# Weight stripes of 512 columns, gates projected in the merge, and a delta net ahead of the attention, in a one-core transformer layer with expert retrieval

## The chip, the cores and the metric

The kernel runs on one core of one Trainium2 chip, as one program of 56,994 profiled instructions. The metric is the device time of one execution in microseconds. A core has five engines with queues of their own: TensorE (PE; its weight loads are listed as PEld), VectorE (DVE), ScalarE (ACT), GpSimd (POOL) and SyncE (SP, which here only issues DMAs). Each engine works off its instructions in a fixed order.

## The reference

One layer over 1024 tokens of width 1024, all in float32. `rmsnorm` stands ahead of each part, and each part is added to `x`.

```python
# 1. token mixing: one input projection, two branches, gates per channel
proj = rmsnorm(x) @ w_in                                   # 1024 x 5640
sb_q, sb_k, sb_v, g_q, g_k, g_v, g_z, g_b, g_a, gate_sb, gate_gdn = split(proj)
o_sb = stick_breaking_attention(sb_q, sb_k, sb_v)          # 8 heads x 64, causal
q, k, v = silu(causal_dwconv(g_q, g_k, g_v)); q, k = l2norm(q), l2norm(k)
o_g  = gated_delta_rule(q, k, v, sigmoid(g_b), decay(g_a)) # 4 heads x 128, chunks, a recurrence
o_g  = rmsnorm(o_g) * silu(g_z)
merged = sigmoid(gate_sb) * (o_sb @ w_sb_up) + sigmoid(gate_gdn) * (o_g @ w_gdn_up)
x = x + merged @ w_mix_out
# 2. cross-attention of 4 heads into 256 memory tokens
x = x + softmax_attention(rmsnorm(x) @ w_cq, rmsnorm(mem) @ w_ckv) @ w_co
# 3. PEER: per token and head the 16 best of 128 x 128 experts, 8 heads
expert, gate = two_stage_topk(rmsnorm(x) @ w_pq, subkeys)  # 128 expert slots per token
x = x + sum(gelu(peer_u[expert] . rmsnorm(x)) * gate * peer_v[expert])
return rmsnorm(x)
```

## The kernel before, in words

**Layout.** Activations are kept transposed, channels on partitions and tokens along the free dimension. A product in float32 is made of three: `split` writes a value as `hi + lo` in the tensor engine's fast float32 format (ACT copies `hi`, DVE or POOL subtracts to get `lo`), and `mm3` multiplies hi by hi, lo by hi and hi by lo, so 24 matmuls for a weight tile of 1024 x 128.

**Weights.** `proj` yields one product per 128 columns of a weight matrix: it loads the tile `raw` (512 KB, three buffers), splits it into `wh` and `wl` (two buffers each) and runs `mm3` into a PSUM tile `pj` (two buffers). The rows of such a tile are 512 bytes long in DRAM. `dense_h` does the same for the transposed expert matrix `peer_ut`.

**Groups.** The tokens go in three groups of 256, 384 and 384 (groups 0, 1, 2). For each group `token_mixing` comes first, then `cross`, then `routing`; the choice of experts (`choose`, long on DVE) follows with the next group's mixing. Inside `token_mixing` the order is: norm; 12 projections of the delta net with the short convolution; SiLU and l2 norm of q, k, v (a `yield` stands here, at which the choice of experts of the group before is put in); 12 projections of the attention (`qT`, `kT`, `vN`); the attention, `stick`, by blocks of 128 queries and 128 keys, two chains of four heads each; 20 projections for the gates, each passed through a sigmoid and stored to `gate_sc` in DRAM; the delta net's chunks (`Chunk.inverse`, `Chunk.scan`); in group 0 `memory_kv`; then the merge, which loads the gates back, lifts both branches (`w_sb`, `w_gdn`) and applies `w_mix`.

**Retrieval.** Of the eight blocks of 128 tokens five fetch their experts' rows by indirect DMAs of POOL, one 512 KB gather for each of 128 slots: `retrieve_u` (row times token on DVE), then `retrieve_v` (sums of rows on PE) or `retrieve_y` (sums on DVE). Seven `row` buffers hold the rows. Blocks 4, 5 and 6 use dense products over all 16,384 experts instead: `spread` turns the chosen gates into a matrix through one-hot tiles `o0`, `o1` (on DVE, and on POOL or ACT), `dense_ahead` makes the first 36 of 128 tiles of activations, and `dense` the rest and the products with `peer_v`. The gathers of later blocks run beside both.

**Order.** The program is written with pools and tiles; a planner with a cost model of its own orders the instructions on each engine ahead of the run, by priority in the order of the program, and puts in the waits. A pool that opens where another was closed waits for that one's tiles. What is written later can be ordered earlier where its operands and buffers are free: the gathers begin during group 1's mixing, the gate projections are spread over the attention.

Of the kernel before, what the change touches and what calls it, by code (L numbers as in the profile page):

```python
# [20 lines left out]
P = 128  # L21
# [5 lines left out]
SH_G, SH_R, SH_S, SH_Z = 3, 0, 6, 0  # L27
# [7 lines left out]
WLS = 2  # L35
SHS = 3
OBS = 12
# [14 lines left out]
def block_kernel(ctx: ExitStack, tc: tile.TileContext, x_t, mem_t, gains, cst, sel, eye, w_in, conv, a_log,  # L52
# [22 lines left out]
    # ---- small helpers  # L75
# [42 lines left out]
    def mix(a, b, ratio):  # L118
        """Steps of a and b in turn, ratio of a for each of b."""
# [21 lines left out]
    # ---- constants  # L141
    cs = const.tile([P, NCST, P], F32, name="cs")
    sp.dma_start(cs, cst)
# [29 lines left out]
    vec.tensor_copy(mk, cs[:, C_SB:C_SB + 2])  # L173
    trir = const.tile([P, 2, P], F32R, name="trir")
# [10 lines left out]
    # ---- scratch in DRAM  # L185
# [4 lines left out]
    gate_sc = dram.tile([len(GROUPS), 20, P, TMAX], F32, name="gate_sc")  # L190
# [35 lines left out]
    def proj(w, col0, ncol, hi, lo, n, kt=KD, share=0):  # L226
        """Yields (tile index, product) for each 128 columns of w, transposed: [columns, tokens]. GpSimd splits
        every share-th tile of w."""
        wv = w.rearrange("(k p) c -> p k c", p=P)
        for c in range(0, ncol, P):  # L230
            raw = wp.tile([P, KD, P], F32, name="raw", bufs=3)
            sp.dma_start(raw[:, :kt], wv[:, :, col0 + c:col0 + c + P])
            wh = wp.tile([P, KD, P], F32R, name="wh")
            wl = wp.tile([P, KD, P], F32R, name="wl", bufs=WLS)
            split(wh[:, :kt], wl[:, :kt], raw[:, :kt], eng=pool if share and c // P % share == share - 1 else vec)
            ps = j_tile()[:, :n]
            mm3(ps, wh, wl, hi, lo, kt)
# [26 lines left out]
    # ---- stick-breaking attention of one 128-query block, four heads at a time, keys on partitions  # L264
    def stick(tmp, kT, vN, qT, sbo, e, qb, t0):
# [3 lines left out]
        after = tmp.tile([P, 512], F32, name=f"after{e}", bufs=1)  # L269
        for kb in range(qb, -1, -1):  # L270
# [6 lines left out]
            # softplus; for large z the logarithm is z itself  # L277
# [26 lines left out]
    # ---- gated delta net over one 128-token chunk, four heads together  # L304
    class Chunk:
# [16 lines left out]
        def prepare(self):  # L322
# [31 lines left out]
            self.qd = self.t4("Q")  # L354
            vec.tensor_mul(self.qd, qc, eg)
# [9 lines left out]
            vec.tensor_mul(self.QT, pQ, dT)  # L365
            yield

        def level(self, l):
            b = self.t4("B" if l % 2 else "D")
            pool.tensor_tensor(b, self.AT, (cs[:, C_LT + l, None, :]).to_broadcast([P, 4, P]), op=OP.mult)  # L370
# [30 lines left out]
            # keys and values with tokens on partitions  # L401
# [15 lines left out]
        def scan(self, S, S2, o):  # L417
            """Recurrence over chunks."""
# [17 lines left out]
    def token_mixing(g, t0, T, x1_where, result):  # L436
# [3 lines left out]
        with ExitStack() as eo:  # L440
            po = open_pool(f"po{g}", 1, where=eo)
            xh, xl = po.tile([P, KD, T], F32R, name="xhi"), po.tile([P, KD, T], F32R, name="xlo")
            sbo = po.tile([P, 4, T], F32, name="sbo")
            qkv = [po.tile([P, 4, T], F32, name=f"gc{i}") for i in range(3)]
            bT = po.tile([4, T], F32, name="bT")
            gT = po.tile([4, T], F32, name="gT")
# [3 lines left out]
            norm_t(xh, xl, po, lambda k: qkv[k // 4][:, k % 4], 0, T)  # L450

            # gated delta net: projections, short convolution
# [9 lines left out]
            # beta and decay logits  # L462
            raw = wp.tile([P, KD, P], F32, name="raw", bufs=3)
# [4 lines left out]
            wh = wp.tile([P, KD, P], F32R, name="wh")  # L468
            wl = wp.tile([P, KD, P], F32R, name="wl", bufs=WLS)
            split(wh, wl, raw)  # L470
            ps = j_tile()[:, :T]
            mm3(ps, wh, wl, xh, xl, KD)
            sigmoid(bT, ps[0:4])
            ya = po.tile([4, T], F32, name="sq", bufs=2)
            yb = po.tile([4, T], F32, name="rs")
# [7 lines left out]
            for i in range(12):  # L483
                d = qkv[i // 4][:, i % 4]
                h = po.tile([P, T], F32, name="sq", bufs=2)
                sigmoid(h, d)
                vec.tensor_mul(d, d, h)
            for i in range(8):
                d = qkv[i // 4][:, i % 4]
                h = po.tile([P, T], F32, name="sq", bufs=2)  # L490
# [3 lines left out]
                h = po.tile([P, T], F32, name="sq", bufs=2)  # L494
# [3 lines left out]
            yield  # L498
            with ExitStack() as es:
# [7 lines left out]
                qT = pn.tile([P, 4, T], F32, name="qT")  # L507
# [16 lines left out]
                for qb in range(t0 // P, t1 // P):  # L524
                    run(*[stick(tmp, kT, vN, qT, sbo, e, qb, t0) for e in range(2)])

            oT = qkv[0]
            with ExitStack() as es:
                tmp = open_pool(f"d2{g}", 2, where=es)
                # output gate and branch gates wait in DRAM  # L530
                n = 0
                for o, m in ((O_Z, 512), (O_GS, 2048)):
                    for i, ps in proj(w_in, o, m, xh, xl, T, share=SH_Z):
# [589 lines left out]
```

## Time and profile before

| what | value |
|---|---|
| median of 3 runs | 3823.45 us (3807.82 to 3836.18) |
| span of the profiled execution | 3821.6 us |
| mean granted PE clock | 0.937 |
| busy: PE, DVE, POOL, ACT | 89%, 75%, 52%, 43% |
| DMA | 1100.56 MB, mean 288 GB/s |

A busy share is the time in which an engine had at least one instruction under way. Matmuls are pipelined and their ends are modelled, so PE can look busy while it waits between the starts of two matmuls; the spacing of starts tells more. "DMA share" is the mean busy share of the core's 16 DMA engines. The profiled execution is one of its own, beside the three timed runs, and its time is the span.

### The profile page before, as it was taken

What the parts mean: (1) busy time and instruction counts of PE and PEld (TensorE: products, weight loads), DVE (VectorE), ACT (ScalarE), POOL (GpSimd) and SP (SyncE); (2) the same over time, 40 slices, a digit from 0 to 9 for tenths busy, and PEclk for the clock granted to TensorE, in tenths of its full rate; (3) what the DMA queues carried; (4) which work ended last, traced back from release to release, by engine and by line L of the source; (5) the groups of instructions that cost most, each with busy time, mean ns of one, the idle gap of its engine ahead of it and who ended that gap; (6) DMA issues with size and microseconds to landing.
All of it is one profiled execution on the core that took longest, in us unless ns stands there. A gap on an engine that the chain in (4) does not pass through costs nothing. (4 is left out here: it accounts for less than half of the span.)

```text
span 3821.6 us, 56994 instructions
## 1 busy us (share of the span) xinstructions
PE 3402.2 (89%) x20621; PEld 2852.3 (75%) x20621; DVE 2852.1 (75%) x5650; ACT 1624.2 (43%) x2992; POOL 1993.3 (52%) x1611
## 2 busy tenths in 40 slices
PE   7998977898889987999978899989769999999995
PEld 6888866787767765767766667878758888888884
DVE  6445699886566799427896667998767888887886
ACT  5754543664313333545523233556633333333333
POOL 1010007666754546467686455788964545544553
PEclk9999988998989988999979899999969999999997
DMA  6537539987899998989878989998999999999996
GB/s 163 147 92 210 151 110 316 332 293 235 290 353 300 347 335 282 307 301 305 263 248 288 345 301 341 305 315 275 325 316 330 340 339 347 339 327 321 360 386 236
DMA packets 745796, 1100.56 MB, mean 288 GB/s; under 512 B 42149, under 2 KB 554533, under 8 KB 742441
## 3 DMA queue, kind: packets, MB, share of 16 engines
q0 software_dynamic: 184320, 671.17, 49.4%
q1 hardware_dynamic: 561192, 425.73, 36.4%
q8 instruction: 163, 2.67, 0.3%
q14 instruction: 121, 0.98, 0.1%
HBM read 1036.60 MB, written 60.16 MB: 287 GB/s over the span
## 5 line engine op out<-in xcount | busy, mean ns | idle before, releaser
L778 POOL DMA_INDIRECT row<-in_peer_u_dram,ix x640 | 818.7, 1279 | 525.5 <-DVE y L83 146.9
L794 DVE CUSTOM_DVE_ANT_0 row<-row,xs 128x1024 f32<-128x1024 f32 x640 | 818.8, 1288 | 123.5 <-DMA row<-in_peer_u_dram,ix 100.9
L223 PE MATMUL pj<-xhi,wh 128*128 128x384 f32 (+1 forms) x1912 | 636.3, 333 | 52.9 <-ACT xhi L77 20.6
L223 PE MATMUL pj<-xhi,wl 128*128 128x384 f32 (+1 forms) x1912 | 637.0, 333 | 26.6 <-POOL wl L89 16.6
L89 DVE TENSOR_TENSOR wl<-raw,wh 128x1024 fp32r<-128x1024 f32 (+1 forms) x420 | 489.9, 1167 | 227.5 <-ACT wh L77 203.7
L778 POOL DMA_INDIRECT row<-in_peer_v_dram,it x384 | 448.6, 1168 | 358.3 <-PE ac L823 169.0
L223 PE MATMUL pj<-xlo,wh 128*128 128x384 f32 (+1 forms) x1912 | 621.4, 327 | 6.4 <-DVE xlo L89 6.4
L77 ACT ACTIVATE wh<-raw 128x1024 fp32r<-128x1024 f32 (+1 forms) x447 | 449.8, 1007 | 276.2 <-PE pj L223 176.5
L778 POOL DMA_INDIRECT row<-in_peer_v_dram,ix x256 | 352.0, 1375 | 346.7 <-DVE y L83 171.9
L223 PE MATMUL pj<-xh,wh 128*128 128x384 f32 x1152 | 399.9, 347 | 44.6 <-ACT h L80 41.6
L223 PEld LDWEIGHTS pj<-xhi,wh 128*128 128x128 f32 x1912 | 371.1, 194 | 89.6 <-ACT xhi L77 26.8
L223 PEld LDWEIGHTS pj<-xhi,wl 128*128 128x128 f32 x1912 | 370.9, 194 | 65.2 <-POOL wl L89 19.5
L223 PE MATMUL pj<-xh,wl 128*128 128x384 f32 x1152 | 398.8, 346 | 4.3 <-POOL wl L89 3.4
L223 PE MATMUL pj<-xl,wh 128*128 128x384 f32 x1152 | 393.1, 342 | 0.0
L223 PEld LDWEIGHTS pj<-xlo,wh 128*128 128x128 f32 x1912 | 369.4, 194 | 23.2 <-issue 10.6
L83 DVE SCALAR_TENSOR_TENSOR y<-row,hh,y 128x1024 f32<-128x1024 f32 x256 | 329.1, 1285 | 14.6 <-DMA row<-in_peer_v_dram,ix 13.1
L823 PE MATMUL ac<-row,sb 128*32 128x256 f32 x3072 | 267.0, 408 | 51.1 <-DMA row<-in_peer_v_dram,it 45.9
L89 POOL TENSOR_TENSOR wl<-raw,wh 128x1024 fp32r<-128x1024 f32 x27 | 66.0, 2443 | 428.1 <-DVE one L758 330.5
L77 ACT ACTIVATE vh<-vr 128x1024 fp32r<-128x1024 f32 x128 | 134.8, 1058 | 322.9 <-PE pj L975 311.6
L223 PEld LDWEIGHTS pj<-xh,wh 128*128 128x128 f32 x1152 | 220.3, 191 | 66.3 <-ACT h L80 56.9
L223 PEld LDWEIGHTS pj<-xh,wl 128*128 128x128 f32 x1152 | 220.7, 192 | 20.0 <-POOL wl L89 4.2
L89 DVE TENSOR_TENSOR vl<-vr,vh 128x1024 fp32r<-128x1024 f32 x128 | 156.5, 1223 | 90.7 <-ACT vh L77 79.3
(453 smaller groups left out, 6583.7 us busy)
## 6 DMA issues: line engine op xcount, KB each, us to landing
raw<-in_w_in_dram SPq DMA_DIRECT2D x132, 512.0 KB
raw<-in_peer_ut_dram SPq DMA_DIRECT2D x128, 512.0 KB
vr<-in_peer_v_dram SPq DMA_DIRECT2D x128, 512.0 KB
raw<-in_w_pq_dram SPq DMA_DIRECT2D x48, 512.0 KB
g_sc<-st SPq DMA_DIRECT2D x12, 2048.0 KB
gm<-g_sc SPq DMA_DIRECT2D x32, 768.0 KB
raw<-in_w_mix_dram SPq DMA_DIRECT2D x24, 512.0 KB
raw<-in_w_cq_dram SPq DMA_DIRECT2D x24, 512.0 KB
```

Of the source, the lines that this page charges most:

```text
L77: return act.activation(o, i, AF.Copy, scale=scale)
L83: return vec.scalar_tensor_tensor(out=o, in0=a, scalar=s, in1=b, op0=op0, op1=op1)
L89: eng.tensor_tensor(lo, src, hi, op=OP.subtract)
L223: pe.matmul(ps, lhsT=a[:, k], rhs=b[:, k], start=i == 0, stop=i == 3 * kt - 1)
L778: pool.indirect_dma_start(out=t, out_offset=None, in_=src, in_offset=bass.IndirectOffsetOnAxis(ap=index, axis=0))
L794: vec.tensor_tensor_reduce(out=t, in0=t, in1=xs, scale=1.0, scalar=0.0, op0=OP.mult, op1=OP.add, accum_out=hh[:, j:j + 1])
L823: pe.matmul(ac[32 * d:32 * d + 32, 256 * w:256 * w + 256], lhsT=sb[:, j], rhs=t[:, 256 * d:256 * d + 256], start=j == 0, stop=j == 31)
```

## The change

All weights of `proj` and of the dense activations are loaded by `stripe`, 512 columns (2 MB) at a time into two buffers, and `halves` splits 128 columns of a stripe. The two lifts read their whole matrix of 2 MB in one load (`proj_up`). The delta net's chunks are computed right behind SiLU and l2 norm, ahead of the attention's projections; its temporary pools are closed then, and `sbo`, `qT` and the running sums of the attention take buffers that have become free. The 20 gate projections move from behind the attention into the merge, and `gate_sc` is gone. Also: `o0`, `o1` have 8 buffers in place of 12, `vh`, `vl` two in place of three, the masks of `level` are bfloat16, the query times decay is kept in place, the logits' projection has 36 columns in place of 128, `h` of `dense_ahead` is stored tile by tile, and the pools `picked` and `yp` open later.

```diff
-    def proj(w, col0, ncol, hi, lo, n, kt=KD, share=0):
-        for c in range(0, ncol, P):
-            raw = wp.tile([P, KD, P], F32, name="raw", bufs=3)
-            sp.dma_start(raw[:, :kt], wv[:, :, col0 + c:col0 + c + P])
-            split(wh[:, :kt], wl[:, :kt], raw[:, :kt], eng=...)
-            mm3(ps, wh, wl, hi, lo, kt)
+    def stripe(w, col0, kt=KD, k0=0, raw=None):
+        raw = raw or wp.tile([P, KD, 512], F32, name="raw", bufs=2)
+        sp.dma_start(raw[:, k0:k0 + kt], w.rearrange("(k p) c -> p k c", p=P)[:, :, col0:col0 + 512])
+        return raw
+    def halves(raw, c, k0=0, kt=KD, n=P, eng=vec):
+        src = raw[:, k0:k0 + kt, c:c + n]
+        wh = wp.tile([P, KD, P], F32R, name="wh")[:, :kt, :n]
+        wl = wp.tile([P, KD, P], F32R, name="wl")[:, :kt, :n]
+        split(wh, wl, src, eng=eng)
+    def proj(w, col0, ncol, hi, lo, n, share=0):
+        for c in range(0, ncol, P):
+            if c % 512 == 0:
+                raw = stripe(w, col0 + c)
+            wh, wl = halves(raw, c % 512, eng=...)
+            mm3(ps, wh, wl, hi, lo, KD)
+    def proj_up(w, hi, lo, n):
+        raw = wp.tile([P, KD, 512], F32, name="raw", bufs=2).rearrange("p (k a) c -> p k (a c)", k=4)
+        sp.dma_start(raw, w.rearrange("(k p) c -> p k c", p=P))
+        for c in range(0, D, P):
+            wh, wl = halves(raw, c, 0, 4)
+            mm3(ps, wh, wl, hi, lo, 4)
...
             yield
+            oT = qkv[0]
+            with ExitStack() as es:
+                tmp = open_pool(f"d2{g}", 2, where=es)
+                (chunks: inverse, then scan)
+            eg.close()
+            sbo = open_pool(f"so{g}", 1, where=eo).tile([P, 4, T], F32, name="sbo")
             with ExitStack() as es:
                 pn = open_pool(f"pn{g}", 1, where=es)
...
-                qT = pn.tile([P, 4, T], F32, name="qT")
+                qT = po.tile([P, 4, T], F32, name="gc1")
+                sums = po.tile([P, 4, T], F32, name="gc2")
                 (projections and attention)
-                for o, m in ((O_Z, 512), (O_GS, 2048)):
-                    for i, ps in proj(w_in, o, m, xh, xl, T, share=SH_Z):
-                        sigmoid(e, ps)
-                        sp.dma_start(gate_sc[g, n, :, :T], e)
-                (chunks: inverse, then scan)
...
-                for h in range(4):
+                for h, pz_ in proj(w_in, O_Z, 512, xh, xl, T):
+                    e = tmp.tile([P, T], F32, name="zr")
+                    sigmoid(e, pz_)
+                    vec.tensor_mul(e, e, pz_)
-                    sp.dma_start(zr, gate_sc[g, h, :, :T])
+                gr = p1.tile([P, KD, T], F32, name="gr")
+                for i, ps in proj(w_in, O_GS, D, xh, xl, T):
+                    sigmoid(x1[:, i], ps)
+                for i, ps in proj_up(w_sb, sbh, sbl, T):
+                    vec.tensor_mul(x1[:, i], x1[:, i], ps)
+                for i, ps in proj(w_in, O_GG, D, xh, xl, T):
+                    sigmoid(gr[:, i], ps)
+                for i, ps in proj_up(w_gdn, oh, ol, T):
+                    vec.tensor_mul(gr[:, i], gr[:, i], ps)
+                    vec.tensor_add(x1[:, i], x1[:, i], gr[:, i])
+                    split(mh[:, i], ml[:, i], x1[:, i])
-                ws, wg = proj(w_sb, 0, D, sbh, sbl, T, 4), proj(w_gdn, 0, D, oh, ol, T, 4)
-                for i in range(KD):
-                        sp.dma_start(gr, gate_sc[g, 4 + 8 * b + i, :, :T])
...
-OBS = 12
+OBS = 8
-                    vh = tmp.tile([P, D], F32R, name="vh", bufs=3)
+                    vh = tmp.tile([P, D], F32R, name="vh")
```

## Rows read from the trace of the kernel before

**Rows 1.** The page: busy us (share of the span) and instructions of each engine.

```profile
PE 3402.2 (89%) x20621; PEld 2852.3 (75%) x20621; DVE 2852.1 (75%) x5650; ACT 1624.2 (43%) x2992; POOL 1993.3 (52%) x1611
```

**Rows 2.** Windows, the mixings: us, busy by engine (count), PE clock, DMA share, GB/s.

```profile
62.00:362.00 300.00, 284.19 (x2208) 265.50 (x2207) 154.05 (x243) 174.76 (x359) 27.41 (x17) 0.99 0.51 143
620.00:1145.00 525.00, 466.11 (x2888) 385.08 (x2889) 380.15 (x606) 229.06 (x415) 347.17 (x266) 0.92 0.89 300
1530.00:2180.00 650.00, 589.45 (x3799) 445.82 (x3797) 421.94 (x633) 275.24 (x501) 427.07 (x341) 0.92 0.88 292
```

**Rows 3.** Windows by stage; busy columns are PE, PEld, DVE, ACT, POOL.

```profile
720.00:905.00 185.00, 181.56 (x1032) 149.26 (x1032) 149.53 (x233) 113.45 (x202) 112.24 (x86) 0.99 0.87 287
905.00:1031.00 126.00, 115.04 (x921) 93.55 (x920) 73.09 (x112) 36.68 (x73) 94.95 (x80) 0.88 0.74 245
1031.00:1145.00 114.00, 89.69 (x543) 67.11 (x542) 71.41 (x122) 27.20 (x45) 65.49 (x57) 0.87 1.01 358
1900.00:2071.00 171.00, 135.00 (x892) 114.55 (x891) 141.07 (x224) 53.66 (x103) 140.66 (x106) 0.83 0.77 249
2071.00:2180.00 109.00, 89.40 (x507) 67.83 (x506) 68.46 (x116) 27.25 (x45) 55.10 (x49) 0.86 1.01 343
2740.00:2820.00 80.00, 35.59 (x152) 31.14 (x152) 57.51 (x115) 30.51 (x88) 70.29 (x67) 0.61 0.79 277
2820.00:3590.00 770.00, 738.79 (x3659) 659.40 (x3660) 625.69 (x742) 267.11 (x363) 370.55 (x277) 0.99 1.00 340
3590.00:3777.00 187.00, 182.42 (x821) 152.06 (x820) 165.54 (x186) 62.18 (x85) 96.43 (x63) 1.00 0.98 353
```

**Rows 4.** Timeline, PE, dense stage and merge: start us, us, instruction.

```profile
1085.35 0.52 PE L223 MATMUL pj<-gc,wl 128*128 128x384 f32 x1
1085.67 0.84 PE L223 MATMUL pj<-gc,wh 128*128 128x384 f32 x2
...
3001.70 0.34 PE L223 MATMUL pj<-xh,wh 128*128 128x384 f32 x1
3001.87 0.34 PE L223 MATMUL pj<-xh,wl 128*128 128x384 f32 x1
```

**Rows 5.** Waits, whole span: us in total, times, longest.

```profile
ACT vh L77 <- PE pj L975: 311.6, 90, 6.0
PEld acc L904 <- POOL o L903: 46.2, 24, 9.6
ACT wh L77 <- DMA raw<-in_w_mix_dram: 30.1, 7, 8.5
```

**Rows 6.** Waits of SP's queue, whole span.

```profile
SPq L538 <- ACT ev L80: 178.4, 40, 10.3
```

**Rows 7.** DMA queues: packets, MB, share; span, then 63:100, then 1031:1145.

```profile
q1 hardware_dynamic: 561192, 425.73, 36.4%
...
q1 hardware_dynamic: 12239, 5.81, 60.6%
...
q0 software_dynamic: 7988, 29.07, 67.3%
```

**Rows 8.** Groups by line, ACT: count, busy us, mean ns, idle before.

```profile
L80 ACT ACTIVATE l<-l 128x512 f32<-128x512 f32 x72 | 45.4, 630 | 1.6
L80 ACT ACTIVATE sq<-sq 128x384 f32<-128x384 f32 (+1 forms) x96 | 44.2, 481 | 0.7
L80 ACT ACTIVATE sh<-z 128x512 f32<-128x512 f32 x72 | 42.9, 596 | 92.3 <-PE z L104 92.1
```

**Rows 9.** Windows of one line: L104 and L823 (PE, PEld), L778 (POOL).

```profile
720.00:905.00 185.00, 94.95 (x497) 63.61 (x497) 0.99 0.87 287
...
1530.00:2180.00 650.00, 81.46 (x1016) 21.99 (x1016) 0.92 0.88 292
...
1145.00:2820.00 1675.00, 816.24 (x679) 0.92 0.90 304
```

**Rows 10.** Tile hh: form, count, ns min/median/max, first and last start.

```profile
L83 DVE SCALAR_TENSOR_TENSOR y<-row,hh,y x256: 1269/1279/2644, 2724.0 to 3810.9; 128x1024 f32<-128x1024 f32 x128
```

More of the change, by code (lines that the diff above doesn't have):

```diff
@@ L139, in run @@
             pass
[L142 to L143 removed]
+    cs = const.tile([P, C_LT, P], F32, name="cs")
+    sp.dma_start(cs, cst[:, :C_LT])
     ident = cs[:, C_ID]
@@ L173, in block_kernel @@
     vec.tensor_copy(mk, cs[:, C_SB:C_SB + 2])
+    lt = const.tile([P, 7, P], BF, name="lt")
+    ct = wp.tile([P, KD, 512], F32, name="raw", bufs=2)[:, :7, :P]
+    sp.dma_start(ct, cst[:, C_LT:])
+    vec.tensor_copy(lt, ct)
     trir = const.tile([P, 2, P], F32R, name="trir")
@@ L268, in stick @@
         oT_ = a_tile()
-        after = tmp.tile([P, 512], F32, name=f"after{e}", bufs=1)
+        after = after[:, 2 * e:2 * e + 2].rearrange("p a b -> p (a b)")
         for kb in range(qb, -1, -1):
@@ L498, in token_mixing @@
             yield
+            oT = qkv[0]
+            with ExitStack() as es:
+                tmp = open_pool(f"d2{g}", 2, where=es)
+                chunks = []
+                for c in range(NB):
+                    cc = slice(c * P, (c + 1) * P)
+                    chunks.append(Chunk(tmp, c, qkv[0][:, :, cc], qkv[1][:, :, cc], qkv[2][:, :, cc], bT[:, cc], gT[:, cc]))
+                run(*[ch.inverse() for ch in chunks])
+                for c, ch in enumerate(chunks):
+                    cur = chunk_no[0] % 2
+                    chunk_no[0] += 1
+                    ch.scan(state[cur], state[1 - cur], oT[:, :, c * P:(c + 1) * P])
+            eg.close()
+            sbo = open_pool(f"so{g}", 1, where=eo).tile([P, 4, T], F32, name="sbo")
             with ExitStack() as es:
@@ L524, in token_mixing @@
                 for qb in range(t0 // P, t1 // P):
[L525 to L531, printed above, removed]
-                for o, m in ((O_Z, 512), (O_GS, 2048)):
-                    for i, ps in proj(w_in, o, m, xh, xl, T, share=SH_Z):
-                        e = po.tile([P, T], F32, name="ev", bufs=2)
-                        sigmoid(e, ps)
-                        if o == O_Z:
-                            vec.tensor_mul(e, e, ps)
-                        sp.dma_start(gate_sc[g, n, :, :T], e)
-                        n += 1
-                chunks = []
-                for c in range(NB):
-                    cc = slice(c * P, (c + 1) * P)
-                    chunks.append(Chunk(tmp, c, qkv[0][:, :, cc], qkv[1][:, :, cc], qkv[2][:, :, cc], bT[:, cc], gT[:, cc]))
-                run(*[ch.inverse() for ch in chunks])
-                for c, ch in enumerate(chunks):
-                    cur = chunk_no[0] % 2
-                    chunk_no[0] += 1
-                    ch.scan(state[cur], state[1 - cur], oT[:, :, c * P:(c + 1) * P])
+                    run(*[stick(tmp, kT, vN, qT, sbo, sums, e, qb, t0) for e in range(2)])
             if g == 0:
@@ L937, in dense_ahead @@
         for r0 in range(0, AHEAD, RG):
-            h = tmp.tile([P, RG, T], F32, name="h")
+            raw = stripe(peer_ut, r0 * P)
             for j in range(RG):
-                dense_h(r0 + j, xh, xl, j_tile()[:, :T], h[:, j], pool if j == 3 else vec)
+                h = tmp.tile([P, T], F32, name="h")
+                dense_h(raw, j, xh, xl, j_tile()[:, :T], h, pool if j == 3 else vec)
+                sp.dma_start(h_sc[:, r0 + j, :T], h)
                 yield
-            sp.dma_start(h_sc[:, r0:r0 + RG, :T], h)
     def dense(xh, xl):
@@ L957, in dense @@
                     sp.dma_start(h, h_sc[:, r0:r0 + RG, :T])
+                else:
+                    raw = stripe(peer_ut, r0 * P)
                 for j in range(RG):
```

78 lines of the change are left out of this document (30 added, 48 removed).

## The prediction, made before the changed kernel was run

> **What bounds the kernel now.** I read the engines' busy times first [rows 1]: TensorE (PE) is busy 89% of the span, more than any other. So the question is where PE isn't doing useful work. For that I read the whole mixings [rows 2], then their stages [rows 3], and beside them the spacing of single matmuls [rows 4]. At the full clock two products of 384 columns start 0.17 us apart; a weight tile of 128 columns has 24 of them, so it costs PE 24 x 0.173 = 4.15 us (2.8 us for the 256 tokens of group 0). The reader is to see three kinds of stage:
> - The dense stage, 2820 to 3777 [rows 3], is PE's own: 739 of 770 us and 182 of 187 busy at the full clock. The change takes no matmul away there.
> - The merges, 1031 to 1145 and 2071 to 2180 [rows 3], hold 16 half tiles and 8 whole ones, 16 x 2.08 + 8 x 4.15 = 66 us of products, and take 114 and 109 us. The granted clock is 0.87 and 0.86 on the mean, matmuls start 0.32 us apart in places [rows 4], which is the lower level of 1.2 GHz, and the DMA share is 1.01. Most of the waits of ACT for tiles of w_mix fall there [rows 5].
> - The gated delta net takes 126 us in group 1 (905 to 1031), but 171 us in group 2 (1900 to 2071), with DVE busy 141 of them [rows 3]: gathered rows are multiplied on DVE at the same time.
>
> The gate projections run under the attention (720 to 905 in group 1), and there PE is busy 98% [rows 3]. The delta net behind them has no projection left to run under it in groups 1 and 2.
>
> **The stripes.** A weight tile of 512 KB is fetched now in 512-byte packets. From 63 to 100 us nothing else moves: 5.81 MB at 60.6% of 16 engines over 37 us, so 5.81 / (0.606 x 37) = 259 GB/s at full share. The gathers, in 4 KB packets, give 29.07 / (0.673 x 114) = 379 GB/s [rows 7]. Packets of 2 KB are not in the trace; their rate lies between, and I take 330. A tile then costs 1.59 us of all engines in place of 2.02. For the 396 whole tiles of the program that is 170 us of DMA time (0 to 252 by the two ends), and the gates' stay in DRAM, 10.5 MB out and back, goes as well: 21 MB at 340 GB/s, 62 us. On the path this counts only where a tile is waited for.
>
> The Trainium skill ("DMA: Bandwidth & Descriptors", Specifications) puts the smallest transfer for line rate at 512 B; by that the stripes would save nothing, and the sum below would end 10 us later. The 259 beside 379 GB/s speaks against it.
>
> A stripe must land whole before its first quarter is split. At the start this costs 2 MB in place of 0.5 MB, 4 to 6 us by the two rates; I take 4, as the norm ahead of it hides some. Later the next stripe has the time of four tiles, 16.6 us, against 2.1 MB / 340 GB/s = 6 us alone and 12 at half the rate beside gathers: hidden, with a cover of only 4 us. The splits read rows of 128 out of 512 columns; I cost that at nothing (the same elements), at most 0.1 us a tile on ACT and DVE, which are not full in these stages.
>
> SP's queue loses 60 stores and 60 loads of gates. A store waits for ACT and holds the weight loads queued behind it, 178 us of such waits in all [rows 6]. PE is busy 98% meanwhile, so I count none by itself.
>
> **The mixing, stage by stage.** Group 1 takes 525 us from 620 to 1145, group 2 takes 650 from 1530 to 2180, group 0 takes 300 from 62 to 362 [rows 2]. What stands ahead of these stretches, projections and the choice of experts, stays. After the change the parts stand in a line: the attention's queries reuse the keys' buffer and its pools the delta net's place, so no projection of the attention can be put away before the scan is done.
> - SiLU and l2 norm, uncovered now: 12 x 3 + 8 x 3 = 60 activations of 0.48 us [rows 8], 29 us.
> - Delta net: 126 us, as in group 1 now (its share of V gathers included). Bounds: 115, its PE time, and 171.
> - The 12 projections of the attention: 12 x 4.15 = 50 us.
> - Attention without gates under it: 24 block steps in group 1, 42 in group 2. A step needs two activations of 0.63 and two of 0.60 us on ACT, 2.45 us (one of each kind is shown, [rows 8]); the attention's line shows 95 us of PE in 720 to 905 for nearly 24 steps, 4.0 a step [rows 9]. I take 3.1, nearer the low end, since modelled matmul ends make PE look longer: 75 and 130 us. Ends: 59 to 95 and 103 to 166.
> - Gates in the merge, 20 x 4.15 = 83; the two lifts, 33; the output projection, 33: 149 us. It needs 18.9 MB of weights, 127 GB/s. Before, 8.4 MB of weights and 3.9 MB of gates had to come in 66 us of products, 186 GB/s. So I expect the full clock.
>
> Group 1: 29 + 126 + 50 + 75 + 149 = 429, and a tenth for waits, 43 (PE is at about 0.9 of the mixings [rows 2]): 472, so 53 us less. Group 2: 484 + 48, and the matmuls of V gathers outside the delta net, about 1016 x (1 - 126 / 575) = 793 at 0.055 us, between half and all of their modelled 0.080 [rows 9], 43: 575, so 75 less. Group 0, without gathers: 284 of 300 us are PE already; the uncovered SiLU (20) stands against a better merge: 0.
>
> **The other edits.** Cross-attention and routing get cheaper weight loads, 10 us less over three groups (0 to 25). The one-hot buffers go from 12 to 8; PE waits for POOL's one-hots already [rows 5], most of it in 2740 to 2820, where PE is busy 36 of 80 us: 15 us more (0 to 40). The value halves go from three buffers to two. In the dense stage ACT waits 312 us for their release already [rows 5] and PE doesn't care; in the last 36 tiles, 187 us with DVE at 0.89, there is little room: 8 us more (0 to 25). The pool of the last rows' sums opens only after the dense products made ahead; its first row comes at 2724 us [rows 10], when those are all but done, so nothing (up to 15). The bfloat16 masks and the 36-column product: nothing, the same counts of instructions.
>
> Sum: -53 - 75 + 4 - 10 + 15 + 8 = -111 us. The profiled span is 3821.6 us and the median of the runs 3823.45, so 3823 - 111 = **3712 us**.
>
> **The rivals.**
> 1. *The gain is handed back in the dense stage.* Gathers go at 679 in 1675 us ahead of it [rows 9], so 111 us less leave some 45 more for a stage whose DMA share is 1.00; each is 0.52 MB / 340 GB/s = 1.5 us, 69 us. The stripes free 92 x 0.43 = 40 there. Net 29 back, or 69 if the stripes free nothing: 3741 to 3781. For it: the share of 1.00 for 770 us. Against: it is PE that the stage waits for.
> 2. *The clock falls in the bare attention.* The merges show what waits do to it. If the attention's 59 + 103 us (ACT's pace) ran half at 1.2 GHz, they would grow by 81 us: 3793. The Trainium skill ("TensorE: Matmul & The Clock Gate", Part 1) says that a PE left idle falls to the lower clock; the trace agrees, with 0.61 from 2740 to 2820 [rows 3].
> 3. *Slower: the delta net meets the gathers.* With nothing else to overlap, DVE's order is filled with gathered rows; the delta net takes in both groups the 171 us that group 2 shows, the 12 projections twice their 50, attention its high end, the merge a tenth of waits. Group 1: 29 + 171 + 100 + 95 + 164 = 559, +34. Group 2: 29 + 171 + 100 + 166 + 164 + 43 = 673, +23. Group 0: the SiLU, +20. One-hots +40. 3823 + 117 = 3940. It decides from the point at which DVE is busy over 80% of the delta net's stretch. For it: this happens from 1900 to 2071. Against: earlier in group 2, where the delta net goes, the gathers are V rows, which DVE doesn't touch.
> 4. *The change doesn't do what it says*: stripes come late. Each of the 15 stripes of a mixing would show 6 us of wait, up to 270 us in all; it shares the chance and the side of rival 3.
>
> **How the numbers follow.** Chances: forecast 0.53, rival 1 0.17, rival 2 0.08, rivals 3 and 4 0.22. About 1%, 38 us, is what a measurement of this kernel can tell from no change. The forecast's own range is 3600 (attention at ACT's pace, half the waits) to 3800. Faster by over 1% (below 3785): 0.46 of the forecast, 0.12 of rival 1, 0.01 of rival 2, 0.59 in all; within 1%: 0.05 + 0.05 + 0.06 + 0.02 = 0.18; slower 0.02 + 0.01 + 0.20 = 0.23. The range 3580 to 3890 leaves out the worse half of rivals 3 and 4 and a gain beyond all bounds.
>
> **What would show it.** Right: merges of 150 to 175 us at a clock of 0.95 or more; ACT's waits for weight tiles nearly gone; the delta net at 110 to 140 us in group 2; a dense stage within 20 us of 957; hardware packets down from 561,192 [rows 7] to about 220,000. Wrong: DVE over 80% in the delta net; a clock below 0.9 in the attention; new PE waits in the dense stage; ACT waiting for a stripe more than a few us.

## The result, and the profile after

The changed kernel takes 3973.39 us (3962.05 to 3976.28), the one before on the same chip 3815.64: ratio 1.0405, interval 1.0366 to 1.0445. It is slower by 158 us by the medians and 154 by the ratio, where 111 us less were predicted. The profiled span is 3960.3 us at a mean granted clock of 0.916, against 3821.6 at 0.937.

The same lines of the profile of the changed kernel: engines of the page, then the hardware's DMA queue (packets, MB, share).

```profile
PE 3448.2 (87%) x20621; PEld 2872.8 (73%) x20621; DVE 2847.1 (72%) x5651; ACT 1633.1 (41%) x2993; POOL 1956.2 (49%) x1611
...
q1 hardware_dynamic: 217656, 404.73, 29.3%
```

The count of matmuls is the one of [rows 1], and PE is "busy" 46 us more: the same work at a lower clock, with waits between. The packets fell from 561,192 [rows 7] to the 220,000 that were foreseen. Windows by stage, columns as in [rows 3]: the attention of group 0; then, for group 1 and for group 2, SiLU with the delta net (from the last weight product ahead of it to the first behind it), the attention's projections (with two of the 20 gate tiles ordered among them), the attention, the merge.

```profile
200.00:218.00 18.00, 14.97 (x79) 10.68 (x78) 6.46 (x10) 12.56 (x23) 0.00 (x0) 0.86 0.16 61
...
665.00:880.00 215.00, 131.09 (x791) 110.43 (x789) 181.03 (x304) 72.23 (x147) 174.42 (x129) 0.71 0.79 264
880.00:962.00 82.00, 78.58 (x480) 67.43 (x478) 35.02 (x48) 24.93 (x38) 44.26 (x33) 0.96 0.86 316
962.00:1086.00 124.00, 109.70 (x733) 63.54 (x728) 79.16 (x118) 62.62 (x112) 91.65 (x79) 0.98 0.84 286
...
1086.00:1253.00 167.00, 165.66 (x1062) 140.63 (x1061) 108.03 (x167) 69.50 (x121) 88.48 (x75) 1.00 0.93 339
...
1639.00:1805.00 166.00, 145.12 (x1175) 105.79 (x1174) 95.31 (x158) 69.22 (x149) 125.94 (x107) 0.88 0.84 284
1805.00:1882.00 77.00, 65.07 (x370) 62.99 (x369) 49.04 (x72) 24.45 (x37) 42.96 (x31) 0.93 0.86 318
1882.00:2138.00 256.00, 213.32 (x1100) 128.13 (x1099) 203.14 (x295) 107.79 (x187) 206.27 (x164) 0.83 0.84 282
...
2138.00:2325.00 187.00, 179.69 (x1116) 148.32 (x1115) 115.42 (x177) 71.01 (x124) 96.88 (x81) 0.99 0.88 316
```

The merges run at the full clock, 1.00 and 0.99, with PE busy in nearly all of their 167 and 187 us. What is far off lies ahead of them: SiLU and delta net of group 1, 215 us with DVE busy 84% and PE's clock at 0.71, and the attention of group 2, 256 us with DVE busy 203. These windows reach from stage to stage; from the first attention step to the last, as the experiments below count it, the attention took 115 us in group 1 and 246 in group 2.

To place the loss, each span is cut in four: up to the load of group 1's tokens, up to that of group 2's, up to the last instruction on group 2's top-16, and the rest. The kernels below stand in this table (the median of the kernel before is that of each chip it was compared on); in the last five the product of a u row is cut to a quarter.

| kernel | group 0 | group 1 | group 2 | rest | span | median of the runs |
|---|---|---|---|---|---|---|
| before | 519 | 894 | 1040 | 1369 | 3822 | 3816 to 3829 |
| after | 547 | 958 | 1086 | 1369 | 3960 | 3973 |
| e1 order | 543 | 968 | 1068 | 1381 | 3960 | 3965 |
| e2 gates | 530 | 953 | 1120 | 1352 | 3955 | 3943 |
| e3 order and gates | 563 | 985 | 1061 | 1362 | 3971 | 3974 |
| e6 after, gathers held | 551 | 906 | 1177 | 1387 | 4021 | 4014 |
| e7 before, 8 one-hots | 518 | 893 | 1046 | 1418 | 3875 | 3880 |
| e8 after, sum on DVE | 552 | 958 | 1072 | 1354 | 3936 | 3937 |
| e9 after, 256 columns, 12 one-hots | 548 | 968 | 1081 | 1313 | 3910 | 3916 |
| e10 before, 256 columns with the wait | 559 | 934 | 1060 | 1385 | 3938 | 3936 |
| e11 before, sum on DVE | 519 | 875 | 1083 | 1398 | 3875 | 3870 |
| e12 = e10 with the sum on DVE | 556 | 934 | 1096 | 1365 | 3951 | 3953 |
| e13 before, wait for a place | 554 | 943 | 1065 | 1403 | 3965 | 3964 |
| e14 before, stripes of 256 | 532 | 880 | 1044 | 1356 | 3812 | 3815 |
| e17 = e9 with cover | 542 | 942 | 1070 | 1340 | 3894 | 3897 |
| e5 before, cut | 520 | 840 | 983 | 1402 | 3745 | 3753 |
| e4 after, cut | 548 | 849 | 1006 | 1368 | 3771 | 3772 |
| e15 gates, cut | 537 | 881 | 1026 | 1360 | 3804 | 3802 |
| e16 order, cut | 545 | 864 | 1025 | 1407 | 3841 | 3850 |
| e18 wait for a place, cut | 551 | 874 | 993 | 1387 | 3805 | 3807 |

The two profiled executions differ by 139 us: +28, +64, +46 in the three groups and nothing behind them. In group 1's delta net most of DVE's time is products of gathered u rows (groups by line, 665 to 880 us):

```profile
L811 DVE CUSTOM_DVE_ANT_0 row<-row,xs 128x1024 f32<-128x1024 f32 x105 | 140.0, 1345 | 27.7 <-DMA row<-in_peer_u_dram,ix 22.0 <-PE pj L445 3.4 <-DMA xs<-xn_sc 1.4
```

The timeline shows the grain (start, duration, instruction; in brackets the idle time before it and what ended it):

```profile
770.98 2.16 DVE L811 CUSTOM_DVE_ANT_0 row<-row,xs 128x1024 f32<-128x1024 f32 x1
...
773.07 1.21 DVE L811 CUSTOM_DVE_ANT_0 row<-row,xs 128x1024 f32<-128x1024 f32 x1
...
774.22 0.68 DVE L400 TENSOR_TENSOR X<-D,cs 128x512 f32<-128x512 f32 x1
...
774.95 0.66 PE L402 MATMUL acc<-cs,X 128*128 128x128 f32 x4 [3.78 <-DVE X L400]
```

The delta net's step on X takes DVE 0.68 us. It stands behind two products of gathered rows (L811), and PE waits 3.78 us for it.

### The profile page after: what moved, and what is told of

Its sections match the earlier page's. It is cut to its first block, busy times and chain, and to the rows that moved or that the text cites. A ratio compares the mean times of both kernels' runs of the same rounds, so it can differ in the third digit from the quotient of the medians.

```text
span 3960.3 us, 56191 instructions
## 1 busy us (share of the span) xinstructions
PE 3448.2 (87%) x20621; PEld 2872.8 (73%) x20621; DVE 2847.1 (72%) x5651; ACT 1633.1 (41%) x2993; POOL 1956.2 (49%) x1611
## 5 line engine op out<-in xcount | busy, mean ns | idle before, releaser
L795 POOL DMA_INDIRECT row<-in_peer_u_dram,ix x640 | 809.5, 1265 | 490.7 <-DVE hh L811 133.7
L811 DVE CUSTOM_DVE_ANT_0 row<-row,xs 128x1024 f32<-128x1024 f32 x640 | 827.8, 1303 | 184.5 <-DMA row<-in_peer_u_dram,ix 171.0
L225 PE MATMUL pj<-xhi,wh 128*128 128x384 f32 (+2 forms) x1912 | 631.7, 331 | 46.9 <-ACT xhi L76 15.2
L225 PE MATMUL pj<-xhi,wl 128*128 128x384 f32 (+2 forms) x1912 | 631.8, 331 | 31.4 <-DVE wl L88 19.2
L225 PE MATMUL pj<-xlo,wh 128*128 128x384 f32 (+2 forms) x1912 | 616.0, 325 | 4.8 <-DVE xlo L88 4.8
L795 POOL DMA_INDIRECT row<-in_peer_v_dram,ix x256 | 335.7, 1312 | 448.6 <-DVE y L82 176.4
L225 PEld LDWEIGHTS pj<-xhi,wh 128*128 128x128 f32 (+1 forms) x1912 | 370.0, 194 | 81.7 <-ACT xhi L76 20.4
L225 PEld LDWEIGHTS pj<-xhi,wl 128*128 128x128 f32 (+1 forms) x1912 | 369.8, 194 | 65.4 <-DVE wl L88 22.2
L225 PEld LDWEIGHTS pj<-xlo,wh 128*128 128x128 f32 (+1 forms) x1912 | 367.2, 193 | 17.6 <-DVE xlo L88 7.9
L76 ACT ACTIVATE vh<-vr 128x1024 fp32r<-128x1024 f32 x128 | 135.7, 1061 | 324.6 <-PE pj L988 320.9
L225 PEld LDWEIGHTS pj<-xl,wh 128*128 128x128 f32 x1152 | 218.9, 190 | 4.6 <-DVE xl L88 2.0
```

Source lines behind the costliest of these rows:

```text
L76: return act.activation(o, i, AF.Copy, scale=scale)
L225: pe.matmul(ps, lhsT=a[:, k], rhs=b[:, k], start=i == 0, stop=i == 3 * kt - 1)
L795: pool.indirect_dma_start(out=t, out_offset=None, in_=src, in_offset=bass.IndirectOffsetOnAxis(ap=index, axis=0))
L811: vec.tensor_tensor_reduce(out=t, in0=t, in1=xs, scale=1.0, scalar=0.0, op0=OP.mult, op1=OP.add, accum_out=hh[:, j:j + 1])
```

## The experiments

Theory A: the delta net, and then the bare attention (with no gate products beside it), run their few DVE steps in one queue with the products of gathered u rows (the prediction's rival 3). Theories B to H stand in the expectations. Ratios are to the kernel before on the same chip.

### The parts of the change

**e1**, the delta net's block put ahead of the attention in the kernel before, the gate projections left behind the attention:

```diff
             yield
+            oT = qkv[0]
+            with ExitStack() as es:
+                tmp = open_pool(f"d2{g}", 2, where=es)
+                (chunks: inverse, then scan)
```

> The kernel before with one part of the change: the gated delta net is put ahead of the attention. Weights still come in tiles of 128 columns, the gates are still projected under the attention and kept in DRAM. Theory A (the order is at fault: in group 1 the delta net now runs while u rows are gathered and multiplied on DVE, and SiLU and l2 norm stand uncovered): the delta net with its SiLU takes over 200 us in group 1 with DVE over 80% busy, and the time is 3880 to 3960 us. Theory B (the gates are at fault: the attention has lost the projections that ran under it): the attention is still covered here, so the time is 3790 to 3840. Theory C (the stripes are at fault): 3790 to 3840 as well.

**e2**, gates alone: the loop that stores to `gate_sc` goes, the merge gets the changed kernel's projections with tiles of 128 columns.

> The kernel before with one part of the change: the gates are projected in the merge and never go to DRAM. The order (attention, then delta net) and the tiles of 128 columns stay. Theory A: the attention is bare but the delta net meets only V gathers; merges grow by 83 us less what the full clock gives, the attention shrinks by 70 to 90; time 3760 to 3840. Theory B: attention at 3.1 us a step or more without cover and merges of 160, so slower: 3860 to 3950. Theory C: 3760 to 3840.

**e3**, both, in tiles of 128 columns.

> The kernel before with both the order and the gates of the change, without its stripes and without its smaller buffers: the delta net first, gates in the merge, weights in tiles of 128 columns. Theory A: 3900 to 3980, the stripes give or take 40 us at most. Theory B: the same 3900 to 3980. Theory C (stripes): 3720 to 3830, as the prediction had it without stripes.

Measured: e1 3965.39 us (1.0381, 1.035 to 1.0411), e2 3942.76 (1.0312, 1.0278 to 1.0345), e3 3973.71 (1.0414, 1.0377 to 1.045). Each half alone costs nearly as much as both. e1 goes A's way, 5 us above its range; e2 lies in B's. C falls: without any stripe e3 is as slow as the changed kernel. Windows of e1 (SiLU and delta net, then attention, group 1) and of e2 (attention, group 2, then group 1):

```profile
667.00:881.00 214.00, 124.00 (x788) 104.85 (x790) 179.33 (x300) 74.81 (x149) 176.54 (x124) 0.72 0.77 261
...
956.00:1108.00 152.00, 152.00 (x860) 120.89 (x859) 63.71 (x85) 92.29 (x161) 30.80 (x25) 1.00 0.44 131
```

```profile
1712.00:1995.00 283.00, 222.69 (x908) 141.21 (x908) 225.10 (x342) 101.88 (x178) 227.74 (x168) 0.71 0.80 263
729.00:881.00 152.00, 125.82 (x495) 82.88 (x494) 118.83 (x191) 63.90 (x110) 107.10 (x83) 0.67 0.77 259
```

In e1 the delta net's stretch is that of the changed kernel, 214 us at a DVE share of 84%. In e2 the attention's steps of group 1, beside u rows, take 152 us without the gates, hardly less than the 162 that they take in the kernel before with gates beside them (721 to 883, last section; [rows 3] has the whole stage): the gate products had been all but free there, and now the merges carry them.

### DVE's queue

**e4** and **e5**, the same edit in the changed kernel and in the one before:

```diff
-            vec.tensor_tensor_reduce(out=t, in0=t, in1=xs, ...
+            vec.tensor_tensor_reduce(out=t[:, :256], in0=t[:, :256], in1=xs[:, :256], ...
```

> The changed kernel, but the product of a gathered u row with the token takes 256 of its 1024 channels (three quarters of that product are left out); every row is still gathered whole. A product costs DVE some 0.45 us in place of 1.21. Theory A with DVE's own time as the price: DVE under 60% in the delta net of group 1, that stretch back from 243 us to under 180, and the total at 3820 to 3890. Theory A with the landing of rows as the price (DVE's queue stands behind a row that hasn't landed): the stretch stays over 215 us, total over 3920. Theories B and C: 3930 to 3975.

> The kernel before with the same cut as in the run on the changed kernel: the product of a gathered u row takes 256 of 1024 channels (three quarters of it left out). There the cut gave back 201 us. Theory A (the changed order makes DVE's time for gathered rows a price on the path): before gains much less, 40 to 110 us, 3710 to 3780, since gate projections stand under its attention and V rows beside its delta net. Theory D (DVE is as much the bound of the kernel before): 170 to 220 us here too, 3600 to 3650, and the contention would explain nothing of the change.

Measured: 3772.02 and 3753.08 us; e5 lies in A's range and D falls, e4 ended below every range. The cut takes 201 us from the changed kernel and 66 to 72 from the one before; by the totals 19 of the 154 us between them remain. With it group 1 differs by 9 us instead of 64, group 2 by 23 instead of 46, and group 0 by the same 28. SiLU and delta net of group 1 in e4, in place of 215 us (in the wider window that the expectation counts, from 650 us on, 151 in place of 243):

```profile
653.00:794.00 141.00, 112.96 (x746) 96.56 (x744) 89.99 (x252) 66.89 (x142) 105.55 (x105) 0.79 0.89 316
```

The rows are as many and as large as before, so in this stretch it is DVE's time that counts, more than their landing (DVE's share, 64%, is above the expected 60).

But the totals make the cut look better than it is. In e5 36 of the 1280 gathers are issued only behind the last dense product, and PE has nothing left to do for 88 us; in the kernel before it is 5 gathers and 42 us, in e4 4 and 30. The windows from the last dense product to the end, of the kernel before and of e5:

```profile
3780.00:3822.00 42.00, 0.00 (x0) 0.00 (x0) 17.06 (x16) 15.11 (x22) 5.61 (x5) 0.52 0.46 162
```

```profile
3657.00:3745.00 88.00, 0.33 (x2) 0.00 (x0) 62.05 (x51) 16.74 (x24) 38.63 (x36) 0.52 0.75 279
```

So e5 has handed back 46 of the 122 us that it gained. Up to the last dense product the changed kernel stands 151 us behind the one before (3930 against 3780), and with the cut still 84 (3741 against 3657): DVE's products of u rows account for 67 of the 151, less than half. Of the 84, 28, 9 and 23 lie in the groups and 24 between the last top-16 and the last dense product. In PE's time, the 151 are 105 us more idle and 46 more for the same matmuls; the 84 are 41 and 43.

**e6**, no u row beside a delta net: `ix` of blocks 0 and 2 gets 0 x the scan's last output added.

```diff
+            vec.tensor_scalar(hold[:, g:g + 1], oT[:, 3, T - 1:T], 0.0, None, op0=OP.mult)
...
+            vec.tensor_scalar(xf, xf, hold[:, g:g + 1], None, op0=OP.add)
```

> The changed kernel, with the row indices of blocks 0 and 2 made to depend on the end of the scan of groups 1 and 2 (three small DVE instructions), so that no u row is gathered beside a delta net. Theory A: from the start of group 1 to its first attention step 300 to 340 us in place of 407, DVE under 70% in the delta net, attention slower by 20 to 40 us since it meets u rows in place of V rows; some 100 rows are gathered later. In all 3880 to 3970. Theory E (the stretch is long because SiLU, l2 norm, choice of experts and delta net form one chain that nothing covers): still over 370 us to the first attention step, total 3970 to 4030.

Measured: 4013.53 us (1.0491, 1.0468 to 1.0515). Windows of group 1: SiLU and delta net, then attention.

```profile
641.00:776.00 135.00, 112.08 (x749) 97.06 (x748) 42.31 (x89) 66.59 (x142) 24.84 (x21) 0.80 0.00 1
...
840.00:985.00 145.00, 112.87 (x473) 74.73 (x472) 116.53 (x183) 57.87 (x99) 107.55 (x79) 0.76 0.80 264
```

From the start of group 1 to its first attention step 289 us in place of 407: by the stretch A again, and E falls. The total lies in E's range all the same, for another reason: the attention now meets the u rows (its steps take 145 us in place of 115), and the rows left over make group 2 91 us longer. Here, keeping the rows away from one chain only gave them to the next.

**e8**, the running sum of `stick` on DVE: `pool.tensor_tensor(after, after, l, ...)` becomes `vec.`.

> The changed kernel with the attention's running sum on DVE in place of POOL, where it queues behind the gathers' descriptor work (ACT waited 60 us for it in group 2's attention). Theory F (POOL's queue sets the pace of the bare attention): group 2's attention from 246 to under 220 us, total 3920 to 3955. Theory A (DVE's queue sets it): DVE gets 36 more instructions of 0.7 us in its fullest stretch, so the same or slower, 3965 to 4000.

Measured: 3937.40 us, 36 less than the changed kernel. But the attention of group 2 went only from 246 to 239 us: ACT no longer waits 60 us for POOL, it waits for PE and DVE instead. By the table 14 us fell in group 2 and 15 behind it. F has the total right and the place wrong. In the kernel before (**e11**) the same edit cost time:

> The kernel before with the attention's running sum on DVE in place of POOL. In the changed kernel this gave back 36 us, little of it in the attentions themselves. If it is the gathers on POOL that it frees: 3785 to 3815. If only a bare attention gains from it (gate projections cover the attention here): 3815 to 3840.

3870.47 us (1.0125, 1.0098 to 1.0151). Neither expectation holds: group 1 gains 19 us, group 2 loses 43 and the rest 29. Why isn't settled.

### One-hots and stripes

**e7**, `OBS = 8` in the kernel before.

> The kernel before with one edit of the change alone: 8 one-hot buffers in place of 12. The prediction's term was 15 us (0 to 40). With that: 3820 to 3845, POOL's wait for free one-hots up from 7 us to some 70. If the smaller buffers cost nothing: 3805 to 3825. If they carry the whole 28 us that the stage lost: 3840 to 3860.

Measured: 3879.83 us (1.0152, 1.0135 to 1.0169), above all three cases and nearly all of it in the one-hot stage: 424 us in place of 374. PE's wait for POOL's one-hots, 46.2 us before [rows 5], in that stage of e7, and then of the changed kernel with POOL's own wait for free buffers:

```profile
PEld acc L904 <- POOL o L903: 81.5, 41, 8.0
```

```profile
PEld acc L921 <- POOL o L920: 72.8, 44, 6.3
POOL o L920 <- PE acc L921: 70.2, 29, 8.6
```

The changed kernel's stage is only 386 us long; no row was gathered from 2600 to 2700 us there, which left POOL to the one-hots. That this is why it lost less is not shown by a run of its own.

**e9**, the changed kernel with stripes of 256 columns and `OBS = 12`.

> The changed kernel with stripes of 256 columns, and in the room that they leave the 12 one-hot buffers of the kernel before. In the kernel before 8 of them cost 55 us; in the changed one the one-hot stage is only 12 us longer than before, because the last rows' gathers start late there and leave POOL free. If the buffers cost those 12 us and packets of 1 KB do nearly what packets of 2 KB do: 3950 to 3985. If the buffers cost 55 us here too, with the gain of the stripes covering 40 of them: 3910 to 3935. If 2 KB packets matter: 3985 to 4010.

Measured: 3915.70 us, 58 less than the changed kernel: the range of the second case. The one-hot stage is 327 us in place of 386, so nearly all of the gain lies there. Which of the two edits made it isn't separated: e3 has 12 one-hots too, without stripes and without the change's smaller edits, and its stage takes 370.

**e10** and **e12**, stripes of 256 in the kernel before, e12 with e8's edit as well. To make room, SiLU's and the l2 norm's tiles had to move to a pool closed ahead of the attention, and two tiles of the dense part got smaller places.

> The kernel before with stripes alone, of 256 columns (512 do not fit beside its pools); order, gates in DRAM and 12 one-hots stay. Against the dense stage's value of the stripes: the comparison of the changed kernel with the one that has 128-column tiles and the same order gave 0 us, with 12 us lost on one-hots in it. Theory A (weights wait for their landing in the merges only): merges shorter by 10 to 25 us each, 3780 to 3815. Theory C (stripes harm, since a tile waits for two to land): 3830 to 3860.

> Both of the last two edits in the kernel before: stripes of 256 columns, running sum on DVE. A version that may beat both kernels: the sum of the two, 3750 to 3805. If either harms, no better than 3820.

Measured: 3936.01 us (1.0303, 1.0281 to 1.0326) and 3952.94 (1.0349, 1.0326 to 1.0372). e10 is above both of its ranges. So either stripes harm or that pool does.

**e13**, the pool alone, no stripes; **e14**, the stripes without the pool (SiLU's tiles rotate through `ev`):

```diff
+            eg = eo.enter_context(ExitStack())
+            pq = open_pool(f"pq{g}", 1, where=eg)
...
-                h = po.tile([P, T], F32, name="sq", bufs=2)
+                h = pq.tile([P, T], F32, name="sq", bufs=2)
...
             yield
+            eg.close()
             with ExitStack() as es:
                 pn = open_pool(f"pn{g}", 1, where=es)
```

> The kernel before with no stripes, but with the one wait that the run with 256-column stripes brought along: the temporary tiles of SiLU and l2 norm lie in a pool of their own that is closed ahead of the attention, so that the attention's first tiles reuse its place and wait for the l2 norm's end. The changed kernel has such a wait too, behind the whole delta net. If the wait is what cost those 120 us: 3890 to 3940, with the first attention step of group 0 some 29 us later and that of group 1 some 40 to 60. If the stripes cost them: 3810 to 3835.

> The kernel before with stripes of 256 columns again, and without that wait: the temporary tiles of SiLU and l2 norm rotate through the two convolution buffers instead. If the wait was at fault: 3780 to 3825. If the stripes were: 3900 to 3940.

Measured: e13 3964.49 us (1.0358, 1.0317 to 1.0399), more than expected, e14 3814.90 (0.9978, 0.996 to 0.9997). Where the attention's tiles reuse the place of the l2 norm's, its projections wait for the whole chain of SiLU and l2 norm, and that wait alone costs 142 us: nearly as much as the change. Wait rows of e13, 640 to 830 us:

```profile
PEld acc L495 <- ACT sq L80: 56.5, 8, 36.9
PE acc L495 <- ACT sq L80: 48.1, 8, 36.6
...
ACT sq L80 <- DVE gc L489: 23.3, 8, 7.0
```

PE stands before the l2 norm's matmul with nothing else to do, ACT waits for DVE's SiLU product. Stripes of 256 columns themselves are worth 0.2% here.

### Cover or queue

**e15**, **e16** and **e18**: e2, e1 and e13 with the cut of e4. **e17**: e9 with 8 of the attention's 12 projections ahead of the delta net.

> The kernel with gates alone (they are projected in the merge, order as before; it lost 123 us), with the cut of the product of a gathered u row to 256 of 1024 channels (three quarters of it left out). The kernel before with the same cut takes 3753 us. Theory A (a bare attention is slow because its few DVE and POOL steps queue behind gathered rows): most of the loss goes, 3750 to 3805. Theory G (the 83 us of gate products a group were free under the attention, whatever its pace, and now stand alone): the loss stays, 3840 to 3890.

> The kernel with the order alone (delta net ahead of the attention, gates under the attention; it lost 146 us), with the same cut to 256 of 1024 channels (three quarters of that product left out). Theory A (the delta net beside u rows): the loss shrinks to under 50 us, 3750 to 3800. Theory H (the wait of the attention's projections for the delta net's place, with SiLU and the choice of experts uncovered, whatever DVE does): 3850 to 3900.

> The kernel before with the wait for the place of SiLU's and the l2 norm's tiles (it cost 142 us), with the product of a gathered u row cut to 256 of 1024 channels (three quarters of it left out). The kernel before with this cut alone takes 3753 us. Theory A (the chain that the attention now waits for is long because its DVE steps queue behind gathered rows): most of the 142 us goes, 3755 to 3805. Theory H (the wait costs the projections that covered the chain, whatever DVE does): 3850 to 3895.

```diff
+            pk = open_pool(f"pk{g}", 1, side="right", where=ek)
+            qT, kn = (pk.tile([P, 4, T], F32, name=n) for n in ("qT", "kn"))
+            for i, ps in proj(w_in, O_SB, 1024, xh, xl, T, share=SH_S):
+                (copies to qT, kn)
+            sp.dma_start(k_sc[:, :, t0:t1], kn)
```

> The changed kernel with 256-column stripes and 12 one-hots (3916 us) and one thing more: the attention's projections of queries and keys, 8 of the 12, are issued ahead of the delta net into tiles of their own, so that they no longer wait for the delta net's place and TensorE has 33 us of products a group beside SiLU, l2 norm and delta net. The keys go through DRAM, as the earlier groups' keys do; the 4 value projections stay behind the delta net. Theory H (a chain has lost its cover): most of 3 x 28 us comes back, 3815 to 3875. Theory A alone (DVE's queue sets the pace of the delta net whatever stands beside it): 33 us are moved from one place to the other and the delta net is as late as before, so 25 to 35 us a group less at most behind it and the same total within 25: 3890 to 3925.

Measured: with the cut, against 3753 us, e15 takes 3801.80 (the top of A's range), e16 3849.99 (the low end of H's) and e18 3807.14 (2 us above A's). The totals hold e5's late end, though; so beside them the loss up to the last dense product, from one profiled execution of each (that of e2 is the slowest of its four runs, 14 us above their median), in us:

| loss of | total | with the cut | up to the last dense product | with the cut |
|---|---|---|---|---|
| the whole change (e4) | 154 | 19 | 151 | 84 |
| the order (e1, e16) | 146 | 97 | 143 | 92 |
| the gates (e2, e15) | 123 | 49 | 138 | 109 |
| the wait (e13, e18) | 142 | 54 | 148 | 84 |

So DVE's queue carries between a fifth and somewhat under a half of each loss, and the larger part stays. That this part is lost cover, products that had run beside a chain and now stand alone, is argued; e17, which puts such products back, is its one direct test. In the attention DVE's queue decides: with the cut the leaving of the gates shortens it by 36 and 67 us in groups 1 and 2 (146 and 281 in e5, 110 and 214 in e15), without the cut by 10 and 4.

e17 takes 3896.81 us (1.0186, 1.0157 to 1.0215), 19 less than e9: group 1 gains 26, group 2 11, group 0 6, and 27 are lost again behind them. The groups give back 43 of the 84 us that H expects, so cover is worth something; the total lies in A's range.

## Why the prediction was wrong

**The step that failed** is the costing of the stages that were moved or uncovered: their times were taken without the row gathers of the new place and, for the attention, as if the gates had made it long (without them it went from 162 to 152 us in group 1 of e2). It has two terms, the second the larger:
- "Delta net: 126 us, as in group 1 now". There it stood beside V rows, which PE multiplies. Moved ahead it meets the u rows of blocks 0 and 1: with SiLU 215 us in group 1 where 155 were predicted. Where the rows are held away it takes 135 (e6), with their cheap product 141 (e4): the term was right but for them. In group 2, beside 53 V rows and 36 u rows, it took 166.
- The attention at "3.1" us a step, 75 and 130 us. That holds in group 0, without gathers: 6 steps in 18 us. From first step to last 24 steps took 115 us in group 1, 4.8 each, and 42 took 246 in group 2, 5.9 each; the high ends, 95 and 166, were no bounds either. DVE's queue is the smaller part of it: with the cut the steps still take 107 and 214 us (e4). In group 1 it is PE: the attention's own matmuls keep it busy for 84 us at a clock of 0.99 (last section), 3.5 a step, and V rows for 19 more. In group 2, with some 100 products of u rows on DVE, ACT waits 60 us for POOL's running sum, but moving that sum to DVE won only 7 (e8); what else sets the pace there stays open.

So group 1 became 215 + 82 + 124 + 167 = 588 us where 472 were predicted, group 2 166 + 77 + 256 + 187 = 686 where 575 were; the 12 projections, with two gate tiles among them, took 82 and 77 in place of 50. Rival 3 had the mechanism for group 1, its point of decision in group 1 (84% against "over 80%") and nearly the time, 3940. That its total comes so near is partly luck: it has the delta net at 200 us with SiLU in both groups, the attention at 95 and 166, too low like the forecast's, and 40 us for one-hots. It got 0.22 together with rival 4, on the argument that the rows there are V rows "earlier in group 2"; group 1, where u rows come first, was not looked at.

**Group 0** was put at 0 and lost 28. It has no rows to meet, as the first gather is issued at 599 us, and the cut changes nothing in it. SiLU, delta net and attention stand there with few products beside them, from 80 to 250 us:

```profile
80.00:200.00 120.00, 102.32 (x754) 92.83 (x755) 36.39 (x69) 57.74 (x129) 21.38 (x16) 0.86 0.15 53
200.00:250.00 50.00, 41.65 (x215) 30.97 (x214) 19.52 (x37) 28.91 (x60) 0.00 (x0) 0.86 0.15 52
```

PE is busy 144 of these 170 us at a clock of 0.86; in the kernel before it was busy 284 of the mixing's 300 at 0.99 [rows 2]. "284 of 300 us are PE already" was so because the chain was covered.

**Right**: the full clock in the merges, though with V rows' products in them they took 167 and 187 us and not 149; the packets; the dense stage, 936 us from its first to its last product with value halves, 938 before, so that the 8 us for the halves' two buffers did not show; ACT's waits for weights, 30 us for w_mix alone before [rows 5] and 2 for all of them after, so that rival 4 did not come; a stripe's rate, 330 GB/s against 348 measured (4.19 MB at 30.1% of 40 us, 60 to 100). One-hots: 15 us, the stage 12 longer in the changed kernel, but 50 in e7. Rival 1 had nothing to hand back here, since nothing was gained ahead of the dense stage; in e5, where 122 us were, 46 came back as late gathers, behind the dense stage and not in it. Rival 2's lower clock did come, 0.83 in group 2's attention and 0.71 in group 1's delta net, but at 246 us and not at ACT's pace.

**The terms of the parts do not add**: 146 for the order and 123 for the gates make 154 together. In the kernel before, three things ran beside each other: a chain of short DVE and ACT steps, the gathered rows and plain products on PE. Each half of the change takes the products from one chain. Why the two losses overlap so far stays open. The small 19 us of the whole change with the cut are mostly e5's late end: up to the last dense product it loses 84, like the halves with their 92 and 109.

## What to carry to other kernels

A stage that is moved costs what it costs in its new place: before taking its duration from the trace, list which background work runs there and on which engine. Work that keeps TensorE busy beside a chain of short steps on other engines can be all but free there, and costs time once it stands behind the chain: the gates are 83 us in groups 1 and 2 each, and moving them cost 123 us in all (e2). A buffer that reuses the place of a chain's temporary tiles costs too, for it orders what was free to overlap (e13). And before the totals of two shortened kernels are compared, see whether both end with the same stage. Of all versions that do the whole work only e14, wider weight loads with no new wait, stood below the kernel before, by 0.2%.

## What the runs showed of the hardware

The granted clock fell where PE had little beside a bare chain. The attention's own 443 matmuls of group 1 took PE 84 us with gate projections beside them (the kernel before) and 118 us in e2 without. In the changed kernel, with no gates but with V rows' products on PE, they took 84 again, and PE was busy 105 of the 115 us. The windows of that one line, in this order:

```profile
721.00:883.00 162.00, 84.36 (x443) 55.66 (x443) 1.00 0.90 298
```

```profile
729.00:881.00 152.00, 118.28 (x444) 79.68 (x443) 0.67 0.77 259
```

```profile
954.00:1069.00 115.00, 83.92 (x443) 54.96 (x442) 0.99 0.79 272
```

So in e2 the bare chain is paid twice: it waits, and its matmuls run in part at 1.2 GHz, 0.67 of the full clock on the mean. Longer packets moved faster at full share, 259 GB/s with 512 bytes, 293 with 1 KB (e14, 63 to 100 us: 6.05 MB at 55.8% of 37 us) and 348 with 2 KB; the 1 KB of e14 bought 0.2% of the time, and what 2 KB are worth by themselves no run separates.
